# A transformer layer on one core: the last norm's scale and bias as matmuls, and expert 30's work in another order

## The chip, the cores and the metric

The kernel runs on one core of a Trainium2 chip. The metric is the device time of one execution in microseconds. Of the engines, PE is TensorE (matmuls and transposes; PEld is its weight load), DVE is VectorE, ACT is ScalarE, POOL is GpSimd, and SP is SyncE, which here does little but issue DMAs. All times below are in us from the start of the span of one profiled execution.

## The reference

One layer over 256 tokens of 1024 channels: `x = LayerNorm(a*x + HybridMixer(x))`, then `x = LayerNorm(a*x + MoE(x))`, in float32. Only the second half matters here:

```
logits = xf @ router_w + router_b            # 256 tokens, 32 experts
top_v, top_i = lax.top_k(logits, 4); gates = softmax(top_v)
# for every expert e, the tokens that chose it:
h = xblk @ w1[e] + b1[e]                     # 1024 -> 2048
gate, upv = split(h); gate = min(gate, 7); upv = clip(upv, -7, 7)
act = (upv + 1.0) * (gate * sigmoid(1.702 * gate))
y  += gates * (act @ w2[e] + b2[e])          # 1024 -> 1024
x = (x - mean) * rsqrt(var + eps) * ln2_g + ln2_b
```

Every expert's weights are read once: 8 MB of `w1` and 4 MB of `w2`, 32 times.

## The kernel before, in words

The first 260 us hold the mixer, the first norm and the router. Then the experts run in a Python loop that is unrolled, `e = 0..30`, with the last one, 31, written out behind it. An expert works on 64 slots. `gemm1` (L1090) multiplies the gathered tokens with `w1` into the PSUM banks `h0` and `h1`, 64 partitions for each half. `hs` is their copy in SBUF (ACT L1096, DVE L1097). `act_steps` (L1173) transposes `hs` on PE into a bank `u`, adds the bias on DVE (L1187), and forms the activation in four more steps on DVE and one on ACT (L1191 to L1196). `gemm2` (L1203) multiplies the result with `w2`; ACT copies it to `ys` (L1209). `scatter` (L1211) multiplies by the gates, transposed by `turn_slots` into `ext`, and adds into the four accumulator banks `acc[t][half]`, which hold the whole layer's output until the end.

Experts run one behind the other: the `gemm2` of expert e-1 and the `scatter` of e-2 stand between the steps of expert e. At `e == SUMS` (8), `residuals()` adds the scaled `x1` into `acc` and `gates_by_expert()` makes `GT`, the gates with the experts on the partitions. The term with `b2` is one product, `gated_biases`: `GT` times `b2r`, four matmuls into `acc`. Before the change it stands in expert 30, and `b2r` is loaded there (L1291).

The weights come through a ring of 23 buffers of 1 MB each. `new_w()` takes the next one; `load_w` (L75) issues one DMA from SP's queue. SP works in program order: a transfer waits until its buffer is free, and until the transfer eight before it has landed, since the queue's completions are counted on eight semaphores in rotation. Expert 31's transfers (class `Last`, L1157) are cut finer at the end: the last 2 MB of `w1` are four transfers of 512 KB, each with one half of the columns for k = 6 and 7, and the last 1 MB of `w2` is two.

PE and, where the code says `PE.`, `DVE.` or `ACT.`, the other engines keep program order (class `Pinned`, whose one call is L48: most rows of PE therefore carry that line, and the tile names tell them apart).

Behind expert 31, `add_sums` (L1386) takes the moments from `acc`, and `normed` (L1403) applies the norm: a mean and a standard deviation for each of two token blocks t, then four pieces (t, h) of 128 x 512. Three of them take two DVE instructions each. The fourth, (0, 1), takes one of ACT and two of POOL. Each piece is stored by one DMA of 256 KB (L1420).

`overflow` (L1227) then reads the largest count of tokens of any expert. Only if it is over 64 does a loop run that works on the crowded experts again and repeats the norm. Before the change this loop reads its weights in blocks into `rws`, one DMA for every matmul.

Of the kernel before, what the change touches and what calls it, by code (L numbers as in the profile page):

```python
# [9 lines left out]
F32 = mybir.dt.float32  # L10
# [5 lines left out]
OP = mybir.AluOpType  # L16
# [5 lines left out]
E = 32  # L22
# [29 lines left out]
def hybrid(ctx: ExitStack, tc: tile.TileContext, A, out, dbg=None):  # L52
# [884 lines left out]
    def u_tile():  # L937
        return ps.tile([128, 512], F32, name="u", bufs=2)
# [4 lines left out]
    def h_tile(c):  # L943
        return ps.tile([128, 512], F32, name=f"h{c}")
# [75 lines left out]

    hs = t1[:, :1024]
    hT = t1[:, 1024:].rearrange("p (j h s) -> p j h s", j=8, h=2)
    wblk = rws.rearrange("p v k e -> p (v k e)")
# [66 lines left out]
    def gemm1(xg, w1):  # L1090

        hp = [h_tile(c) for c in range(2)]
        for k, c, half in w1.order:
            PE.matmul(hp[c][half * 64:(half + 1) * 64], xg[:, k],
                             w1(k, half * 2 + c), start=(k == 0), stop=(k == 7), skip_group_check=True)
        nc.scalar.copy(hs[:, :512], hp[0])  # L1096
        nc.vector.tensor_copy(hs[:, 512:], hp[1])  # L1097

    class Weights:


        def __init__(self, e, one=False):
            self.e, self.one = e, one
            self.order = ([(k, c, half) for c in range(2) for half in range(2) for k in range(8)] if one else
                          [(k, c, half) for k in range(8) for c in range(2) for half in range(2)])

        def block(self, name, k, c):
            cs = slice(c * 512, (c + 1) * 512)
            if name == 'moe_w1':
                src = A[name][ds(self.e, 1), k * 128:(k + 1) * 128, cs]  # L1110
            else:
                src = w2v[ds(self.e, 1), :, k // 2, k % 2, cs]
            nc.sync.dma_start(wblk, src.rearrange("e p f -> p (e f)"))
            return wblk

    class First(Weights):
        def load(self):
            self.w = [load_w(w1v[self.e][:, k:k + 1, :], 1, 2048) for k in range(8)]
            return self

        def __call__(self, k, c):
            if self.one:
                return self.block('moe_w1', k, c)
            return self.w[k][:, 0, c * 512:(c + 1) * 512]

    class Second(Weights):
        def load(self):
            self.w = [load_w(w2v[self.e][:, q], 2, 1024) for q in range(4)]
            return self

        def __call__(self, k, c):
            if self.one:
                return self.block('moe_w2', k, c)
            return self.w[k // 2][:, k % 2, c * 512:(c + 1) * 512]

    class Last:
# [36 lines left out]
    def act_steps(bias, a, g=None, banks=None):  # L1173


        bv = bias.rearrange("p (h j) -> p j h", h=2)
        pieces = [slice(q * 4, (q + 1) * 4) for q in range(2)]
        js = slice(0, 8)
        if g is not None:
            js = slice(4 * g, 4 * g + 4)  # L1180
            pieces = [js]
        for i, piece in enumerate(pieces):
            n = piece.stop - piece.start
            p = (banks[i] if banks else u_tile())[:, :n * 128]
            for j in range(n):
                PE.transpose(p[:, j * 128:(j + 1) * 128], pair(hs, piece.start + j), ident)
            nc.vector.tensor_tensor(hT[:, piece], p.rearrange("p (j h s) -> p j h s", j=n, h=2),  # L1187
                                    bv[:, piece, :].unsqueeze(3).to_broadcast([128, n, 2, SLOTS]), op=OP.add)
        yield
        gate, up = hT[:, js, 0, :], hT[:, js, 1, :]  # L1190
        nc.vector.tensor_scalar(gate, gate, LIMIT, None, op0=OP.min)  # L1191
        sg = hs[:, js.start * 128:js.start * 128 + (js.stop - js.start) * 64].rearrange("p (j s) -> p j s", s=64)
        nc.scalar.activation(sg, gate, AF.Sigmoid, scale=1.702)
        nc.vector.tensor_scalar(up, up, LIMIT, -LIMIT, op0=OP.min, op1=OP.max)
        nc.vector.tensor_tensor(sg, sg, gate, op=OP.mult)
        nc.vector.scalar_tensor_tensor(a[:, js], up, 1.0, sg, op0=OP.add, op1=OP.mult)  # L1196

    def act(*args, **kw):
        for _ in act_steps(*args, **kw):
# [2 lines left out]

    def gemm2(a, w2):  # L1203
        yp = u_tile()
        for k, c, half in w2.order:
            if c == 0:
                PE.matmul(yp[half * 64:(half + 1) * 64, :], a[:, k], w2(k, half),
                                 start=(k == 0), stop=(k == 7), skip_group_check=True)
        nc.scalar.copy(ys, yp)  # L1209

    def scatter(gT, first=False):  # L1211
# [21 lines left out]
    def overflow(stores):  # L1233

        with ExitStack() as behind:
            for i in stores:
                behind.enter_context(tc.issue_after(i))
            most = nc.values_load(cnts[0:1, E:E + 1], min_val=0, max_val=T)
        with tc.If(most > SLOTS):
            with tc.For_i(0, E, 1) as ei:  # L1240
                ce = nc.values_load(cnts[0:1, ds(ei, 1)], min_val=0, max_val=T)
                with tc.If(ce > SLOTS):
                    be = lp.tile([128, 16], F32, name="be")
                    nc.vector.tensor_copy(be.unsqueeze(2), b1T[:, :, ds(ei, 1)])
# [37 lines left out]
    for e in range(E - 1):  # L1282
# [3 lines left out]
        w1 = First(e).load()  # L1286
        if 0 < e < E - 2:
            w2 = Second(e - 1).load()
        if e == E - 2:
            b2r = new_w()[:E, :D]  # L1290
            nc.sync.dma_start(b2r, A['moe_b2'])  # L1291
        if e:
# [17 lines left out]
        elif e < E - 2:  # L1310
# [17 lines left out]
            if e == SUMS:  # L1328
                scatter(*late)
                late = None  # L1330
                residuals()
                GT = gates_by_expert()
            if e == E - 3:

                scatter(*late)
                gemm2(a, Second(e).load())
        else:
            gT = turn_slots(buf, u_tile())
            scatter(prev[1])
            steps = act_steps(b1T[:, :, e], a_main)  # L1340
            next(steps)
            gTn = turn_slots(1 - buf, h_tile(0), S)

            gated_biases(GT, b2r)
            for _ in steps:
                pass
            a = a_main
            w2 = Second(e).load()
            last = Last().load()
            gemm2(a, w2)  # L1350
# [47 lines left out]
                          start=False, stop=True, skip_group_check=True)  # L1398
        add_sums(st, c)
    ov = out[0].rearrange("(t p) d -> p t d", p=128)  # L1400
    y = new_w().rearrange("p (t d) -> p t d", t=2)

    def normed(st):  # L1403
        stats = [statistics(st[t]) for t in range(2)]
        nm = lp.tile([128, 1], F32, name="nm")

        def norm2(t, h, tail=None):
            (mu, rs), c = stats[t], slice(h * 512, (h + 1) * 512)
            d = y[:, t, c]
            out_q = nc.sync  # L1410
            if tail is None:
                out_q = nc.scalar
# [3 lines left out]
            else:  # L1416
# [3 lines left out]
            return out_q.dma_start(ov[:, t, c], d).ins  # L1420

        def scales():
            for _, rs in stats:
                DVE.reciprocal(rs, rs)
            DVE.scalar_tensor_tensor(nm, stats[0][0], -1.0, stats[0][1], op0=OP.mult, op1=OP.mult)

        return [norm2(0, 0, scales), norm2(0, 1)] + [norm2(1, h, lambda: None) for h in range(2)]

    overflow(normed(st))

# [22 lines left out]
```

## Time and profile before

| | us |
|---|---|
| median of 3 runs | 1203.75 |
| the runs | 2316.03, 1203.75, 1200.88 |
| the profiled execution's own time | 1199.88 |
| its span (first to last instruction) | 1198.0 |
| busy: PE, DVE, ACT, POOL | 1134.0, 347.0, 208.2, 64.4 |
| DMA | 449.37 MB, mean 375 GB/s |

Busy times are sums over the whole span, which has stages with different limits, so the table says little by itself. The chain of waits, followed back from the last instruction, names DMA for 51% and PE for 45% of the span. Matmul ends are modelled, so a PE that reads as busy all the time may hold short waits.

### The profile page before, as it was taken

Reading aid. Unit: us, or ns where it says so; the run is one execution under the profiler, and the core shown is the slowest. Engines: PE = TensorE matmul, PEld = TensorE weight load, DVE = VectorE, ACT = ScalarE, POOL = GpSimd, SP = SyncE. Lnnn points to the kernel's source line nnn. Section 1 sums busy time; section 2 is a strip of 40 time slices with the busy share of each in tenths; the row PEclk is TensorE's granted clock in tenths of the full one; section 3 lists DMA queues with packets and bytes.
Section 4 is the critical chain, followed back from the end, with each engine's and each line's share of the span. In section 5 each row is a group of like instructions: output and inputs, shape, how many; then the busy total and the mean of one; then the engine's idle time right before and its main releaser. Section 6 shows DMA issues by size and latency. Waiting matters only on the chain.

```text
span 1198.0 us, 15607 instructions
## 1 busy us (share of the span) xinstructions
PE 1134.0 (95%) x6464; PEld 584.8 (49%) x6465; DVE 347.0 (29%) x700; ACT 208.2 (17%) x491; POOL 64.4 (5%) x106
## 2 busy tenths in 40 slices
PE   8999999999999999999999898989898989899994
PEld 7998889984434334343433333333333333334332
DVE  6679777472112111111121111111111111111014
ACT  5115554532101011010101000101010101011001
POOL 1010001311000000000000000000000000000000
PEclk9999999999999999999999999999999999999998
DMA  9994466869999999999999999999999999999993
GB/s 247 327 321 142 129 205 250 306 231 419 424 424 424 424 425 423 425 423 425 423 425 422 426 423 425 423 424 423 426 423 425 424 424 425 425 424 425 419 406 153
DMA packets 100358, 449.37 MB, mean 375 GB/s; under 512 B 11108, under 2 KB 44826, under 8 KB 51514
## 3 DMA queue, kind: packets, MB, share of 16 engines
q1 hardware_dynamic: 99774, 447.51, 92.6%
q8 instruction: 52, 0.85, 0.3%
q10 hardware_dynamic: 508, 0.81, 0.2%
q14 instruction: 24, 0.20, 0.1%
HBM read 447.25 MB, written 1.05 MB: 374 GB/s over the span
## 4 chain that ended last, share of the span: by engine, by line
DMA 51%; PE 45%; DVE 2%; SPq 1%; ACT 1%; issue 0%; ACTq 0%; DVEq 0%
DMA w<-in_moe_w_dram 50%; PE h L48 16%; PE u L48 8%; PE mm L87 4%; PE mm L88 4%; PE mm L89 4%; PE acc L48 3%; DMA w<-in_w_in_dram 1%; PE sc L641 1%; PE yps L686 1%; PE ptp L677 1%; PE sc L48 1%; PE mm L48 1%; DVE w L48 0%; DMA x<-in_x_dram 0%
## 5 line engine op out<-in xcount | busy, mean ns | idle before, releaser
L48 PE MATMUL h<-w,t 128*64 128x512 f32 (+1 forms) x1472 | 328.0, 588 | 31.2 <-DMA w<-in_moe_w_dram 30.4
L48 PEld LDWEIGHTS h<-w,t 128*64 128x64 f32 x1472 | 99.4, 136 | 249.0 <-issue 161.4
L48 PE MATMUL u<-w,t 128*64 128x512 f32 x960 | 212.9, 595 | 0.0
L1097 DVE COPY t<-h 128x512 f32<-128x512 f32 x31 | 21.4, 691 | 512.8 <-PE h L48 512.8
L48 PE MATMUL h<-w,rws 128*64 128x512 f32 x640 | 146.2, 603 | 11.2 <-DMA w<-in_moe_w_dram 11.0
L48 PEld LDWEIGHTS u<-w,t 128*64 128x64 f32 x960 | 66.2, 137 | 124.4 <-issue 118.3
L48 PEld LDWEIGHTS h<-w,rws 128*64 128x64 f32 x640 | 43.8, 138 | 108.7 <-issue 76.1
L87 PE MATMUL mm<-xh,ws 128*128 128x256 f32 x336 | 96.8, 288 | 0.0
L1096 ACT COPY t<-h 128x512 f32<-128x512 f32 x31 | 18.1, 585 | 447.5 <-PE h L48 447.5
L88 PE MATMUL mm<-xl,ws 128*128 128x256 f32 x336 | 95.0, 283 | 0.0
L89 PE MATMUL mm<-xh,ws 128*128 128x256 f32 x336 | 94.9, 283 | 0.0
L82 DVE TENSOR_TENSOR ws<-w,ws 128x1024 fp32r<-128x1024 f32 (+1 forms) x64 | 73.2, 1148 | 11.8 <-ACT ws L81 11.0
L1074 POOL TENSOR_TENSOR ext<-ext,G 128x128 f32<-128x128 f32 x62 | 27.1, 456 | 815.8 <-PE h L48 797.2
L48 PE MATMUL acc<-t,ext 64*128 64x512 f32 (+1 forms) x264 | 63.9, 602 | 1.6 <-ACT t L1393 0.9
L87 PEld LDWEIGHTS mm<-xh,ws 128*128 128x128 f32 x336 | 64.3, 191 | 1.0 <-issue 0.8
L88 PEld LDWEIGHTS mm<-xl,ws 128*128 128x128 f32 x336 | 64.4, 192 | 0.0
L89 PEld LDWEIGHTS mm<-xh,ws 128*128 128x128 f32 x336 | 64.3, 191 | 0.0
L1196 DVE SCALAR_TENSOR_TENSOR t<-t 128x512 f32<-128x512 f32 (+1 forms) x32 | 21.6, 675 | 144.0 <-PE u L48 143.8
L1209 ACT COPY t<-u 128x512 f32<-128x512 f32 x31 | 18.2, 586 | 175.3 <-PE u L48 175.3
L1187 DVE TENSOR_TENSOR t<-u,b1T 128x512 f32<-128x512 f32 x35 | 24.0, 690 | 78.3 <-PE u L48 78.3
L48 PEld LDWEIGHTS acc<-t,ext 64*128 64x128 f32 x264 | 22.7, 186 | 41.1 <-issue 27.8
L81 DVE CAST ws<-w 128x1024 fp32r<-128x1024 f32 (+1 forms) x47 | 29.7, 642 | 23.0 <-PE mm L89 15.6
(338 smaller groups left out, 1085.6 us busy)
## 6 DMA issues: line engine op xcount, KB each, us to landing
w<-in_moe_w_dram SPq DMA_DIRECT2D x381, 1024.0 KB
w<-in_w_in_dram SPq DMA_DIRECT2D x22, 1024.0 KB
w<-in_w_up_dram SPq DMA_DIRECT2D x6, 1024.0 KB
w<-in_cmp_w_dram SPq DMA_DIRECT2D x4, 1024.0 KB
w<-in_w_o_dram SPq DMA_DIRECT2D x4, 1024.0 KB
w<-in_w_in_dram SPq DMA_DIRECT2D x6, 512.0 KB
w<-in_moe_w_dram SPq DMA_DIRECT2D x6, 512.0 KB
out_dram<-w SPq DMA_DIRECT2D x3, 256.0 KB
```

The costliest lines, as they stand in the source:

```text
L48: return lambda *a, **k: self.tc.keep_in_program_order(f(*a, **k))
L81: copy(hi, src)
L82: return sub.tensor_tensor(lo, src, hi.bitcast(F32), op=OP.subtract).ins
L87: pe.matmul(p, ah, bh, start=first, stop=False, **kw)
L88: pe.matmul(p, ah, bl, start=False, stop=False, **kw)
L89: pe.matmul(p, al, bh, start=False, stop=last, **kw)
L1074: nc.gpsimd.tensor_tensor(SG[:, t], S[:, t, x:x + 1].to_broadcast([128, 2, SLOTS]), gsrc[:, t].unsqueeze(2).to_broadcast([128, 2, SLOTS]), ...
L1096: nc.scalar.copy(hs[:, :512], hp[0])
L1097: nc.vector.tensor_copy(hs[:, 512:], hp[1])
L1187: nc.vector.tensor_tensor(hT[:, piece], p.rearrange("p (j h s) -> p j h s", j=n, h=2), bv[:, piece, :].unsqueeze(3).to_broadcast([128, n, ...
L1196: nc.vector.scalar_tensor_tensor(a[:, js], up, 1.0, sg, op0=OP.add, op1=OP.mult)
L1209: nc.scalar.copy(ys, yp)
```

## The change

It has four parts.

1. The closing norm. Each bank that holds a piece of the result is first filled with the bias row by a matmul of the identity with `b2`; DVE forms `(acc - mean) * g2` for each piece; a matmul with a diagonal matrix of the inverse deviations scales it and adds it to the bank; ACT (and DVE for a quarter) copies the bank to SBUF. `y` lies in `t1` and no longer in a ring buffer. The last piece is copied and stored in two halves, so there are five stores, all from SP's queue, and none from ACT's. POOL has no work in it any more.
2. Expert 30. The transposes of `act_steps` stand ahead of the scatter of expert 29; the activation is made in two halves; the `gated_biases` are no longer here.
3. Expert 8. `b2r` is loaded here, and `gated_biases` stands here, behind `residuals()`.
4. The crowded experts load their weights through the ring, with the same `load()` as the others.

```diff
-        for k, c, half in w1.order:
-            PE.matmul(hp[c][half * 64:(half + 1) * 64], xg[:, k],
-                             w1(k, half * 2 + c), start=(k == 0), stop=(k == 7), skip_group_check=True)
+        for k in range(8):
+            for c in range(2):
+                for half in range(2):
+                    PE.matmul(hp[c][half * 64:(half + 1) * 64], xg[:, k],
+                              w1(k, half * 2 + c), start=(k == 0), stop=(k == 7), skip_group_check=True)
...
-                        gemm1(xg[0], First(ei, True))
+                        gemm1(xg[0], First(ei).load())
                         a = act(be, xg[0])
-                        gemm2(a, Second(ei, True))
+                        gemm2(a, Second(ei).load())
...
-        if e == E - 2:
+        if e == SUMS:
             b2r = new_w()[:E, :D]
             nc.sync.dma_start(b2r, A['moe_b2'])
...
-                GT = gates_by_expert()
+                gated_biases(gates_by_expert(), b2r)
...
             gT = turn_slots(buf, u_tile())
+            a = a_main
+            steps = [act_steps(b1T[:, :, e], a, c, DVE) for c in range(2)]
+            for c in range(2):
+                next(steps[c])
             scatter(prev[1])
-            steps = act_steps(b1T[:, :, e], a_main)
-            next(steps)
             gTn = turn_slots(1 - buf, h_tile(0), S)
-
-            gated_biases(GT, b2r)
-            for _ in steps:
-                pass
-            a = a_main
+            for c in range(2):
+                for _ in steps[c]:
+                    pass
...
-    y = new_w().rearrange("p (t d) -> p t d", t=2)
+    y = t1.rearrange("p (t d) -> p t d", t=2)
 
     def normed(st):
+
+        banks = [[u_tile(), u_tile()], [h_tile(0), h_tile(1)]]
+        for t in range(2):
+            for h in range(2):
+                PE.matmul(banks[t][h], ident, b2[:, h * 512:(h + 1) * 512], start=True, stop=False,
+                          skip_group_check=True)
         stats = [statistics(st[t]) for t in range(2)]
...
-                ACT.activation(d, acc[t][h], AF.Identity, bias=nm, scale=rs)
-                nc.gpsimd.tensor_tensor(d, d, g2[:, c], op=OP.mult)
-                nc.gpsimd.tensor_tensor(d, d, b2[:, c], op=OP.add)
...
-                DVE.scalar_tensor_tensor(d, acc[t][h], mu, g2[:, c], op0=OP.subtract, op1=OP.mult)
-                tail()
-                DVE.scalar_tensor_tensor(d, d, rs, b2[:, c], op0=OP.mult, op1=OP.add)
...
+        def centered(t, h):
+            c = slice(h * 512, (h + 1) * 512)
+            DVE.scalar_tensor_tensor(y[:, t, c], acc[t][h], stats[t][0], g2[:, c], op0=OP.subtract, op1=OP.mult)
+
+        def scaled(t, h, n, copies):
+            for i, copy in enumerate(copies):
+                c = slice(h * 512 + i * n, h * 512 + (i + 1) * n)
+                p = banks[t][h][:, i * n:(i + 1) * n]
+                PE.matmul(p, diag[t], y[:, t, c], start=False, stop=True, skip_group_check=True)
+                copy(y[:, t, c], p)
+                stores.append(nc.sync.dma_start(ov[:, t, c], y[:, t, c]).ins)
+
+        centered(0, 0)
+        for t in range(2):
+            rs = stats[t][1]
+            DVE.reciprocal(rs, rs)
+            DVE.tensor_scalar(diag[t], ident, rs, None, op0=OP.mult)
+        for t, h in ((0, 1), (1, 0), (1, 1)):
+            centered(t, h)
+        for t, h in ((0, 0), (0, 1), (1, 0)):
+            scaled(t, h, 512, [ACT.copy])
+        scaled(1, 1, 256, [DVE.tensor_copy, ACT.copy])
+        return stores
```

PE's order in expert 30, from the gates' transposes behind `gemm1` to `gemm2`. `t_3267` holds `ys` and the activation, `t_3268` holds `hs`, `ext` the gates, `acc_*` are the four accumulators. Before:

```order
L48 MATMUL u<-ident,ext 128x128 x2
L48 MATMUL acc_3275<-t_3267,ext 128x512
L48 MATMUL acc_3276<-t_3267,ext 128x512
L48 MATMUL acc_3466<-t_3267,ext 128x512
L48 MATMUL acc_3467<-t_3267,ext 128x512
L48 MATMUL u<-ident,t_3268 128x128 x8
L48 MATMUL h_7042<-ident,ext 128x128 x2
L48 MATMUL acc_3275<-w,GT 128x512
L48 MATMUL acc_3276<-w,GT 128x512
L48 MATMUL acc_3466<-w,GT 128x512
L48 MATMUL acc_3467<-w,GT 128x512
L48 MATMUL u<-w,t_3267 64x512 x16
```

The same place now, in the changed kernel, on PE:

```order
L48 MATMUL u<-ident,ext 128x128 x2
L48 MATMUL u<-ident,t_3268 128x128 x8
L48 MATMUL acc_3275<-t_3267,ext 128x512
L48 MATMUL acc_3276<-t_3267,ext 128x512
L48 MATMUL acc_3466<-t_3267,ext 128x512
L48 MATMUL acc_3467<-t_3267,ext 128x512
L48 MATMUL h_7046<-ident,ext 128x128 x2
L48 MATMUL u<-w,t_3267 64x512 x16
```

The eight transposes of `hs` moved ahead of the four scatter matmuls, and the four matmuls with `GT` are gone from here. They stand in expert 8 now, where PE's order reads (`x_76` with `ident_a` are the residuals, `G` the gates):

```order
L48 MATMUL acc_3275<-x_76,ident_a 128x512
L48 MATMUL acc_3276<-x_76,ident_a 128x512
L48 MATMUL acc_3466<-x_76,ident_a 128x512
L48 MATMUL acc_3467<-x_76,ident_a 128x512
L48 MATMUL u<-ident,G 32x128 x2
L48 MATMUL acc_3275<-w,GT 128x512
L48 MATMUL acc_3276<-w,GT 128x512
L48 MATMUL acc_3466<-w,GT 128x512
L48 MATMUL acc_3467<-w,GT 128x512
```

PE runs these four right behind the transposes of `G`, and expert 9's `gemm1` follows them. At the end of the program PE's order is now this, where before the four scatter matmuls of 256 columns were its last work:

```order
L48 MATMUL acc_3275<-t_3267,ext 128x256
L48 MATMUL acc_3276<-t_3267,ext 128x256
L48 MATMUL acc_3466<-t_3267,ext 128x256
L48 MATMUL acc_3467<-t_3267,ext 128x256
L48 MATMUL u<-w,ident 128x512 x2
L48 MATMUL h_7231<-w,ident 128x512
L48 MATMUL h_7232<-w,ident 128x512
L48 MATMUL u<-t_3268,ext 128x512 x2
L48 MATMUL h_7231<-t_3268,ext 128x512
L48 MATMUL h_7232<-t_3268,ext 128x256 x2
```

Behind the last scatter stand four matmuls that put the bias in, and then the scaling ones: three of 512 columns and two of 256.

## Rows read from the trace of the kernel before

**Rows 1.** The page's second part: the span in 40 equal slices of 30 us. DMA is the mean busy share of the 16 DMA engines in tenths (9 is 90% or more), GB/s what they moved.

```profile
DMA  9994466869999999999999999999999999999993
GB/s 247 327 321 142 129 205 250 306 231 419 424 424 424 424 425 423 425 423 425 423 425 422 426 423 425 423 424 423 426 423 425 424 424 425 425 424 425 419 406 153
```

**Rows 2.** The chain that ended last, in order of time: start, length, what.

```profile
499.44 5.62 PE acc L48 x16
...
533.23 19.71 DMA w<-in_moe_w_dram
...
1119.05 20.30 DMA w<-in_moe_w_dram
...
1145.00 3.62 PE acc L48 x8
...
1160.99 8.86 PE h L48 x40
...
1191.11 0.98 DVE w L48
```

**Rows 3.** Waits from 533 to 1139 us, of SP's queue and of PE: who waited, for whom, us in total, times, longest.

```profile
SPq L75 <- DMA w<-in_moe_w_dram: 507.3, 243, 2.9
SPq L75 <- PE h L48: 3.5, 12, 0.4
...
PE h L48 <- DMA w<-in_moe_w_dram: 40.4, 80, 0.7
```

**Rows 4.** SP's queue near the end: start and length of three issues by the timeline, and the semaphore waits of the stores' line, which begin at 1167.9.

```profile
1155.41 1.45 SPq L1157 DMA_DIRECT2D w<-in_moe_w_dram  x1
...
1165.30 0.66 SPq L1157 DMA_DIRECT2D w<-in_moe_w_dram  x1
1166.58 0.55 SPq L1157 DMA_DIRECT2D w<-in_moe_w_dram  x1
...
L1420 SPq EVENT_SEMAPHORE  x3: 17/17/17, 1167.9 to 1190.8; - x3
```

**Rows 5.** PE's timeline in expert 31's `gemm1`: k = 0 and 1 (16 records), the scatter of expert 30 (8), then k = 2 to 5 with both column halves and k = 6, 7 with the first (40 records). A float32 matmul leaves two records.

```profile
1155.47 3.60 PE L48 MATMUL h<-w,t 128*64 128x512 f32 x16
1159.01 1.99 PE L48 MATMUL acc<-t,ext 64*128 64x512 f32 x8
1160.92 8.91 PE L48 MATMUL h<-w,t 128*64 128x512 f32 x40
```

**Rows 6.** Two stretches near the end: length, then for PE, PEld, DVE, ACT and POOL the busy time and the count, then the granted clock, the DMA share and GB/s.

```profile
1166.00:1170.00 4.00, 3.84 (x18) 1.32 (x14) 0.00 (x0) 0.13 (x1) 0.00 (x0) 1.00 1.03 411
...
1178.00:1180.00 2.00, 2.00 (x22) 1.24 (x20) 0.13 (x1) 0.00 (x0) 0.00 (x0) 1.00 0.36 126
```

**Rows 7.** The timeline in expert 8 (the residuals, the copy of `GT`) and the starts of two `gemm1` that lie two experts apart.

```profile
501.36 3.70 PE L48 MATMUL acc<-x,ident_a 128*128 128x512 f32 x8
505.32 0.41 DVE L1224 COPY GT<-u 32x256 f32<-32x256 f32 x1 [5.82 <-PE u L48]
...
531.60 13.96 PE L48 MATMUL h<-w,t 128*64 128x512 f32 x64
...
583.55 13.95 PE L48 MATMUL h<-w,t 128*64 128x512 f32 x64
```

**Rows 8.** The timeline of the activation: the transposes of expert 30, and, of expert 31, which is done in halves before too, the bias, the sigmoid and the last step of one half.

```profile
1143.56 1.23 PE L48 MATMUL u<-ident,t 128*128 128x128 f32 x8
...
1171.29 0.69 DVE L1187 TENSOR_TENSOR t<-u,b1T 128x512 f32<-128x512 f32 x1 [23.03 <-PE u L48]
...
1172.43 0.42 ACT L1193 ACTIVATE t<-t 128x256 f32<-128x256 f32 x1 [1.97 <-DVE t L1191]
...
1173.34 0.43 DVE L1196 SCALAR_TENSOR_TENSOR t<-t 128x256 f32<-128x256 f32 x1
```

**Rows 9.** The timeline of the end: an ACT copy of 512 columns and one of 256 from PSUM, the last scatter, the end of the moments, the first piece's subtraction, the last store.

```profile
1169.87 0.58 ACT L1366 COPY t<-h 128x512 f32<-128x512 f32 x1 [13.60 <-PE h L48]
...
1183.66 0.37 ACT L1393 COPY t<-h 128x256 f32<-128x256 f32 x1 [2.25 <-PE h L48]
...
1184.09 1.14 PE L48 MATMUL acc<-t,ext 64*128 64x256 f32 x8 [0.47 <-ACT t L1393]
...
1186.16 0.38 DVE L48 BATCH_NORM_AGGREGATE bn_mv<-st 128x2 f32<-128x24 f32 x2
...
1186.69 0.75 DVE L48 SCALAR_TENSOR_TENSOR w<-acc,bn_mv,w 128x512 f32<-128x512 f32 x1
...
1192.11 0.33 SPq L1420 DMA_DIRECT2D out_dram<-w  x1
```

**Rows 10.** SP behind the last store: its wait at the branch, and the nine semaphores that it goes through after it (shortest/median/longest ns, first and last start).

```profile
SPq L1239 <- SPq L1239: 2.5, 1, 2.5
...
L1239 SPq EVENT_SEMAPHORE  x9: 17/17/17, 1196.1 to 1196.7; - x9
```

**Rows 11.** Three stretches in the columns of Rows 6; the granted clock is the third number from the right.

```profile
1082.00:1086.00 4.00, 4.00 (x30) 2.93 (x26) 0.69 (x1) 1.76 (x3) 0.00 (x0) 1.00 1.01 426
1086.00:1090.00 4.00, 4.00 (x13) 1.27 (x14) 0.00 (x0) 0.58 (x1) 0.00 (x0) 0.57 1.02 424
...
1188.00:1190.00 2.00, 0.00 (x0) 0.00 (x0) 1.97 (x3) 0.52 (x1) 1.32 (x2) 0.62 0.34 131
```

**Rows 12.** The page's sixth part, the stores that SP issued in the whole execution.

```profile
out_dram<-w SPq DMA_DIRECT2D x3, 256.0 KB
```

More of the change, by code (lines that the diff above doesn't have):

```diff
@@ L1022, in hybrid @@
     hT = t1[:, 1024:].rearrange("p (j h s) -> p j h s", j=8, h=2)
-    wblk = rws.rearrange("p v k e -> p (v k e)")
     a_main = t2[:, 1024:1536].rearrange("p (j s) -> p j s", j=8)
@@ L1096, in gemm1 @@
         nc.scalar.copy(hs[:, :512], hp[0])
         nc.vector.tensor_copy(hs[:, 512:], hp[1])
[L1099 to L1114, printed above, removed]
@@ L1116, in hybrid, with of_expert, __init__ @@
-    class First(Weights):
+    def of_expert(v, e):
+        return v[e] if isinstance(e, int) else v[ds(e, 1)].rearrange("e p r f -> (e p) r f")
+    class First:
+        def __init__(self, e):
+            self.src = of_expert(w1v, e)
         def load(self):
-            self.w = [load_w(w1v[self.e][:, k:k + 1, :], 1, 2048) for k in range(8)]
+            self.w = [load_w(self.src[:, k:k + 1, :], 1, 2048) for k in range(8)]
             return self
         def __call__(self, k, c):
-            if self.one:
-                return self.block('moe_w1', k, c)
@@ L1124, in __call__, with __init__ @@
             return self.w[k][:, 0, c * 512:(c + 1) * 512]
-    class Second(Weights):
+    class Second:
+        def __init__(self, e):
+            self.src = A['moe_w2'][e] if isinstance(e, int) else A['moe_w2'][ds(e, 1)].rearrange("e f d -> (e f) d")
+            self.src = self.src.rearrange("(q p r) d -> q p r d", p=128, r=2)
         def load(self):
-            self.w = [load_w(w2v[self.e][:, q], 2, 1024) for q in range(4)]
+            self.w = [load_w(self.src[q], 2, 1024) for q in range(4)]
@@ L1129, in load @@
             return self
         def __call__(self, k, c):
-            if self.one:
-                return self.block('moe_w2', k, c)
             return self.w[k // 2][:, k % 2, c * 512:(c + 1) * 512]
@@ L1171, in second, with act_steps @@
                           start=(j == 0), stop=(j == 7), skip_group_check=True)
-    def act_steps(bias, a, g=None, banks=None):
+    def act_steps(bias, a, g=None, vec=nc.vector, banks=None):
         bv = bias.rearrange("p (h j) -> p j h", h=2)
@@ L1186, in act_steps @@
                 PE.transpose(p[:, j * 128:(j + 1) * 128], pair(hs, piece.start + j), ident)
-            nc.vector.tensor_tensor(hT[:, piece], p.rearrange("p (j h s) -> p j h s", j=n, h=2),
+            vec.tensor_tensor(hT[:, piece], p.rearrange("p (j h s) -> p j h s", j=n, h=2),
                                     bv[:, piece, :].unsqueeze(3).to_broadcast([128, n, 2, SLOTS]), op=OP.add)
@@ L1190, in act_steps @@
         gate, up = hT[:, js, 0, :], hT[:, js, 1, :]
-        nc.vector.tensor_scalar(gate, gate, LIMIT, None, op0=OP.min)
+        vec.tensor_scalar(gate, gate, LIMIT, None, op0=OP.min)
         sg = hs[:, js.start * 128:js.start * 128 + (js.stop - js.start) * 64].rearrange("p (j s) -> p j s", s=64)
         nc.scalar.activation(sg, gate, AF.Sigmoid, scale=1.702)
-        nc.vector.tensor_scalar(up, up, LIMIT, -LIMIT, op0=OP.min, op1=OP.max)
-        nc.vector.tensor_tensor(sg, sg, gate, op=OP.mult)
-        nc.vector.scalar_tensor_tensor(a[:, js], up, 1.0, sg, op0=OP.add, op1=OP.mult)
+        vec.tensor_scalar(up, up, LIMIT, -LIMIT, op0=OP.min, op1=OP.max)
+        vec.tensor_tensor(sg, sg, gate, op=OP.mult)
+        vec.scalar_tensor_tensor(a[:, js], up, 1.0, sg, op0=OP.add, op1=OP.mult)
     def act(*args, **kw):
@@ L1204, in gemm2 @@
         yp = u_tile()
-        for k, c, half in w2.order:
-            if c == 0:
+        for k in range(8):
+            for half in range(2):
                 PE.matmul(yp[half * 64:(half + 1) * 64, :], a[:, k], w2(k, half),
-                                 start=(k == 0), stop=(k == 7), skip_group_check=True)
+                          start=(k == 0), stop=(k == 7), skip_group_check=True)
         nc.scalar.copy(ys, yp)
@@ L1400, in hybrid @@
     ov = out[0].rearrange("(t p) d -> p t d", p=128)
-    y = new_w().rearrange("p (t d) -> p t d", t=2)
+    y = t1.rearrange("p (t d) -> p t d", t=2)
     def normed(st):
-        stats = [statistics(st[t]) for t in range(2)]
[L1405 to L1412, printed above, removed]
-                ACT.activation(d, acc[t][h], AF.Identity, bias=nm, scale=rs)
-                nc.gpsimd.tensor_tensor(d, d, g2[:, c], op=OP.mult)
-                nc.gpsimd.tensor_tensor(d, d, b2[:, c], op=OP.add)
-            else:
-                DVE.scalar_tensor_tensor(d, acc[t][h], mu, g2[:, c], op0=OP.subtract, op1=OP.mult)
-                tail()
-                DVE.scalar_tensor_tensor(d, d, rs, b2[:, c], op0=OP.mult, op1=OP.add)
[L1420 to L1427, printed above, removed]
@@ new lines, in normed @@
+        banks = [[u_tile(), u_tile()], [h_tile(0), h_tile(1)]]
[3 more added lines that the diff above has]
+                          skip_group_check=True)
+        stats = [statistics(st[t]) for t in range(2)]
+        diag = [ext[:, 512 + t * 128:640 + t * 128] for t in range(2)]
+        stores = []
+        def centered(t, h):
+            c = slice(h * 512, (h + 1) * 512)
+            DVE.scalar_tensor_tensor(y[:, t, c], acc[t][h], stats[t][0], g2[:, c], op0=OP.subtract, op1=OP.mult)
```

## The prediction

> **What bounds the kernel now.** I began with the page's slices. From about 290 us on, the DMA engines are busy in every slice at 420 to 425 GB/s, and only the last slice falls off [rows 1]. The expert stage is thus fed by a stream of weights that is never idle. The chain of waits then says who ends it [rows 2]. Up to 533 PE is on the chain, in expert 8 too (499.44). From 533.23 the chain runs on landings of weights, one after the other, until 1139.35 (1119.05 + 20.30). Behind that it is PE without a break, then DVE at the very end. So by the chain the last 52 us belong to PE, and work taken from PE there should shorten the kernel.
>
> I do not trust that reading, because a chain shows one path and hides a second one that is as long. So I looked at when the weights of expert 31 land. SP may not issue a transfer before the one eight places earlier has landed, so its issue times are landing times. The two last issues, at 1165.30 and 1166.58, mark the landing of w1 for k = 5 and of the first piece of k = 6, 7; the first store's semaphore wait at 1167.9 marks the second piece [rows 4]. PE reaches that second piece in its block that starts at 1160.92: 40 records in 20 pairs; the 0.59 us of one record's own length off the 8.91, over 19 steps, is 0.44 a pair, and the 17th pair starts at 1160.92 + 16 x 0.44 = 1167.9 [rows 5]. **PE and the stream arrive at the same moment.** The stream itself is full there, with a share of 1.03 at 1166 to 1170, and still moves weights at 1178 to 1180 [rows 6]. The kernel has two bounds in its last 52 us, level with each other, and the change shortens one of them.
>
> **The change, part by part.** *Expert 30.* The four `GT` matmuls go: 3.62 us of PE's chain [rows 2]. The transposes come before the scatter, so the activation runs beside it. PE then has: transposes 1.23 from about 1141.7 [rows 8], a scatter of 1.9 (1159.01 to 1160.92, [rows 5]), 0.3 of gate transposes, free at about 1145.1. The first half of the activation starts as its four transposes end, at about 1142.4. DVE adds both biases (2 x 0.69), and from there to the half's last step it is about 1.7 us, as in expert 31: bias done at 1172.0, last step over at 1173.34 + 0.43 [rows 8]. So it is ready at about 1145.5 and `gemm2` starts there, instead of 1145.00 + 3.62 = 1148.6. PE gains 3.1 us. That is the whole gain on offer, and it lasts until PE meets the stream. w1 for k = 1 landed at 1155.41 [rows 4]; PE, 3.1 us early, would want it at 1154.1 (half of the 3.60-us block behind 1155.47 - 3.1, [rows 5]) and loses 1.3 us to it. Pieces k = 2 to 5 take the next part, and k = 6 is the end: with or without the gain PE starts it at 1167.9. I take **0.0 us** (bounds: 3.1 less if PE's side were the only one; nothing more).
>
> *Expert 8.* PE gets the same four matmuls, which by the residuals, of the same size, are 3.70 less an overlap, say 3.5 [rows 7], and waits for the copy of `GT`, 0.41 [rows 7], with two handovers: about 4.2 in all. This is while PE is on the chain. But two `gemm1` two experts apart start 52.0 us apart [rows 7], 26.0 each, while an expert's 12 MB take 12 x 1.0486 MB / 424 GB/s = 29.7. PE gains 3.7 us an expert on the stream, so it is back at the stream's heels little more than one expert later, and then waits for it 40.4 us in all up to 1139 [rows 3]. That is the cover: 0. If it were gone, 4.2. The ring is no obstacle either: between 533 and 1139 SP waited 507.3 us on landings and 3.5 on PE [rows 3], so buffers come free in time. `b2r` is 0.13 MB; it leaves the stream at expert 30 and joins it at expert 8, where it is as full [rows 1]: 0, at best 0.3 (0.13 MB / 424 GB/s) if it falls into a gap.
>
> *The closing norm.* Before: moments end at about 1186.5, the last store is issued at 1192.11 [rows 9]. Now PE carries four bias matmuls behind the last scatter, and the scaling of 4 x 512 columns behind them. The nearest row is the residuals, 128 x 128 on 512 columns in float32, four in 3.70 with the drain and about 3.5 without [rows 7]. The scatter ends at 1184.09 + 1.14 = 1185.2 [rows 9]; 3.5 + 3.7 make 1192.4. DVE is not late: from 1186.6 four subtractions at 0.75 and some small steps end near 1190.2, and the diagonal is there before the bias is in. Behind the last quarter stands an ACT copy of 256 columns at 0.37 and two handovers [rows 9]: the last store goes out at 1192.8, **0.7 us later**. ACT's copies of 512 columns at 0.58 keep pace with PE's 0.9. The waits for ring semaphores ahead of DVE's first subtraction go with `y`, which frees DVE and not PE. Bounds: PE's bias matmuls wholly hidden, about -2.8; PE at half its clock, +7.2 (a rival below).
>
> *After the last store* SP reads the count and branches; it stands 2.5 us at the branch and leaves it at 1196.1 [rows 10], 4.0 after its issue. I move this with the issue. [...]
>
> *The crowded experts.* SP issued three stores in the whole execution [rows 12]; the loop would have issued more. It doesn't run, before or after: 0.
>
> **Sum:** 1199.9 + 0.0 + 0.0 + 0.7 = 1200.6 against the profiled execution. The two runs near it that had no profile, 1200.88 and 1203.75, lie 1.0 and 3.9 above; I add 1.0 and forecast **1201.5 us**, against a median before of 1203.75 which is the higher of them. About 2% (24 us) is what a measurement of this kernel can tell from no change; no part here comes near it.
>
> **The rivals.** *A, PE's side alone sets the end.* Then the 3.1 us go through: 1201.5 - 3.1 = 1198.4. For it speaks the chain, on PE from 1139.35 on [rows 2]; against it the semaphore at 1167.9 [rows 4]. It would decide if in other executions the weights of k = 6 landed 3 us sooner. 0.14.
>
> [...] From 1086 to 1090 the granted clock was 0.57, most of it at the lower level, behind a stretch of narrow matmuls [rows 11] that by the records had PE busy all the time. The tail before the norm has narrow matmuls and short waits too. If the clock falls as the bias matmuls begin, 7.2 us of them become 14.4: 1208.7. It decides if the clock falls before 1192; until now it fell at 1188 to 1190, with PE idle since 1185.2 [rows 9, 11], which the new work prevents. 0.06. [...]
>
> *C, slower: the 4.2 us at expert 8 stay.* PE is on the chain there, and if the ring were short the stream would stop for it: 1205.7. Against it SP's 3.5 us [rows 3]. 0.05.
>
> The forecast's own case gets 0.72; 0.03 is left for things of which no row speaks.
>
> **Range and chances.** The forecast with the scatter of the runs (1200 to 1204.5) and A reach from 1197.5; C reaches to 1205.5. B is left out. All named cases lie within 2%: same 0.95, faster 0.02, slower 0.03.
>
> **What would show it.** Expert 30: transposes ahead of the scatter, `gemm2` about 3 us earlier against the last landing of expert 30's w1. Then PE waits for weights in expert 31, before k = 1 and before k = 6, about 3 us in sum, and the chain of waits goes on DMA up to about 1168. The norm: PE on the chain for 7 us behind the last scatter, at a clock of 1.00, POOL with nothing. Expert 8: a landing on the chain one or two experts later than 533. I am wrong if PE shows no such waits and the span is near 1195, if the clock falls in the norm, or if the last store goes out earlier against the last scatter than before.

## The result and the profile after

| | before | after |
|---|---|---|
| median of 6 runs each, us | 1200.90 | 1208.46 |
| ratio, 95% interval | | 1.0061 [1.0048, 1.0074] |
| profiled execution: its own time, its span, us | 1199.88, 1198.0 | 1208.99, 1207.2 |
| share of the chain: PE, DMA | 45%, 51% | 53%, 44% |

(The ratio leaves out one run of before, of 2316 us, which the median of six still counts.) The change is called "same" at 2%, but it is 7.6 us slower, more than twice what its interval is wide. 1201.5 was forecast, with a range up to 1205.5. The page's slices of the changed kernel already show where the time went:

```profile
DMA  8994466769999999999999999999999999999993
GB/s 243 319 324 141 126 203 251 304 235 420 420 422 420 421 420 421 408 420 420 422 420 421 421 422 420 421 420 421 421 420 421 421 420 420 421 421 421 421 413 142
```

The stream of weights is as unbroken as in [rows 1], but between its ends it moves 420 to 422 GB/s, in one slice 408, where it moved 422 to 426. A table of two stretches says it with more weight (length, then busy time and count of PE, PEld, DVE, ACT and POOL, then granted clock, DMA share, GB/s). After:

```profile
300.00:450.00 150.00, 149.89 (x754) 60.87 (x752) 25.85 (x45) 16.28 (x36) 5.31 (x12) 1.00 1.01 421
...
500.00:1100.00 600.00, 558.82 (x2680) 212.51 (x2678) 87.11 (x152) 57.21 (x125) 17.69 (x40) 0.99 1.01 421
```

and the same stretches of the kernel before:

```profile
300.00:450.00 150.00, 149.88 (x754) 60.84 (x752) 25.82 (x45) 16.29 (x36) 5.31 (x12) 1.00 1.01 424
...
500.00:1100.00 600.00, 560.41 (x2700) 212.24 (x2698) 86.35 (x151) 56.64 (x124) 17.71 (x40) 1.00 1.01 424
```

From 300 to 450 us both kernels execute the same instructions: what the change moves begins behind that. The engines' busy times and counts agree, the DMA share is 1.01 in both, and yet the stream is slower by 3 GB/s. So no instruction that the change adds, drops or moves is the cause.

What it is worth is read from SP's queue (start, length, line, count). In the changed kernel the first weights of the experts and the last two transfers of expert 31's `w2` are issued here (the first of these two waits for the landing of `w1` for k = 5, eight places earlier):

```profile
195.61 1.31 SPq L75 DMA_DIRECT2D w<-in_moe_w_dram  x3
```

```profile
1173.69 1.85 SPq L1147 DMA_DIRECT2D w<-in_moe_w_dram  x2
```

Before, the second place is at 1165.30 [rows 4], and the first here:

```profile
194.04 1.30 SPq L75 DMA_DIRECT2D w<-in_moe_w_dram  x3
```

The stream begins 1.6 us later and ends 8.4 us later, so from the first place to the second it takes 978.1 us instead of 971.3, 6.8 more. From about 290 to 1165 us, 3 of 424 GB/s are 875 x 3 / 424 = 6.2 us, and the view rounds these rates to 1 GB/s. The load of `b2r` in expert 8, which makes one slice 408, has no part in it: after_pad below loads `b2r` there too, and its stream takes 971.3 us. The 1.6 lies in the mixer, where the kernels below scatter: they have that first issue anywhere from 193.3 to 196.8, and the latest is one with a fast stream (after_bd256).

Behind the stream the chain of waits is the one that the prediction described (start, length, what):

```profile
1132.82 19.90 DMA w<-in_moe_w_dram
1152.78 20.89 DMA w<-in_moe_w_dram
1173.72 4.61 PE h L48 x16
...
1192.56 1.13 PE acc L48 x8
1193.70 1.91 PE u L48 x4
1195.61 1.72 PE h L48 x4
1197.33 1.72 PE u L48 x4
1199.04 1.30 PE h L48 x4
1200.85 0.71 PE h L48 x2
```

Before, the last landing on it ended at 1139.35 and PE had the rest [rows 2]. Now landings hold it until 1173.67 (in after_pad below until 1165.65), and PE starts k = 5 of expert 31 the moment they end, with k = 6 and 7 behind it. The whole delay of the stream thus reaches the end.

### The profile page after: what moved, and what is told of

Read it like the earlier page. It is cut to its first block, busy times and chain, and to the rows that moved or that the text cites. A ratio compares the mean times of both kernels' runs of the same rounds, so it can differ in the third digit from the quotient of the medians.

```text
span 1207.2 us, 15641 instructions
## 1 busy us (share of the span) xinstructions
PE 1146.2 (95%) x6482; PEld 590.2 (49%) x6483; DVE 345.8 (29%) x704; ACT 209.6 (17%) x495; POOL 61.0 (5%) x104
## 4 chain that ended last, share of the span: by engine, by line
PE 53%; DMA 44%; DVE 1%; ACT 0%; issue 0%; SPq 0%; ACTq 0%; DVEq 0%
DMA w<-in_moe_w_dram 43%; PE h L48 20%; PE u L48 10%; PE mm L87 4%; PE mm L88 4%; PE mm L89 4%; PE acc L48 3%; DMA w<-in_w_in_dram 1%; PE sc L641 1%; PE yps L686 1%; PE mm L48 1%; PE ptp L677 1%; PE sc L48 1%; PE ptp L48 0%; DMA x<-in_x_dram 0%; PE ptp L87 0%
```

## The experiments

**Where the 3 GB/s went.** The norm no longer makes one small tile, and that is the only thing I found that the change alters for the work before 450 us:

```diff
-        nm = lp.tile([128, 1], F32, name="nm")
```

The tile has 4 bytes a partition and takes 32. Its pool, `late`, lies at the right end of SBUF and is filled from there, so everything to the left of it moves up by 32 bytes: the buffers of `ring_x` (203520 to 203552, bytes from a partition's start), `t2` and `t1`, and those of `ring_c` (146176 to 146208). All of them began at multiples of 256 bytes. Of the 23 buffers of the ring, 5 are `ring_c`, 2 `ring_x`, 8 `ring_a` (start 128 behind a multiple of 256 in both kernels), and 4 each `ring_b` and `ring_d` (64 behind in both). My theory was that these starts set the speed of the stream; the rival, that some part of the new order does. Two kernels put the question both ways: the changed kernel with an unused tile in the old one's place, and the kernel before with one tile more.

```diff
     lp = ctx.enter_context(tc.tile_pool(name="late", bufs=1, side="right"))
+    lp.tile([128, 1], F32, name="pad")
```

On the change (after_pad):

> The changed kernel with one unused tile of 4 bytes a partition (32 with its padding) in the pool at the right end of the SBUF. It puts the seven ring buffers of the pools ring_c and ring_x, and t1 and t2, back to the addresses of the kernel before (multiples of 256 bytes instead of 32 bytes behind one); nothing else differs from the change. Theory (addresses): the stream of weights goes back from 421 to 424 GB/s between 500 and 1100 us, its last landing comes some 8 us sooner, and the time is 1200 to 1201.5 us, ratio to before 0.999 to 1.001, with the closing norm's 0.7 us the only thing left. Rival (the work itself: b2r and the four matmuls in expert 8, or the norm, slow the stream): it stays at 1208, ratio 1.006, and 421 GB/s.

On the kernel before (before_off32):

> The kernel before with one more unused tile of 32 bytes a partition in the same pool, so that ring_c, ring_x, t1 and t2 lie 32 bytes below a multiple of 64, with none of the change's work. Theory (addresses): 1207 to 1209 us, ratio 1.006, at 421 GB/s between 500 and 1100 us. Rival (the work itself): 1200.9 us, ratio 1.000, at 424 GB/s.

Then the same place moved by 64 bytes (`lp.tile([128, 56], F32, name="pad")` in the changed kernel, after_off64), and all 23 buffers put at multiples of 256 (after_all256: after_pad with a tile of 128 bytes ahead of `ring_a` and one of 64 in the constants):

```diff
+    front = ctx.enter_context(tc.tile_pool(name="front", bufs=1, side="left"))
+    front.tile([128, 32], F32, name="pad_a")
     ring_a = ctx.enter_context(tc.tile_pool(name="ring_a", bufs=NA, side="left"))
...
+    consts.tile([128, 16], F32, name="pad_b")
```

> The changed kernel with 224 bytes a partition of unused tile in the same pool: ring_c and ring_x then begin 64 bytes behind a multiple of 256, as ring_b and ring_d do in every kernel so far. If 64 bytes are what counts: as with the 32-byte tile, 1200 to 1201.5 us, 424 GB/s. If 256 bytes count, 1206 to 1209 us, about 421 GB/s. Rival (the work itself): 1208.

> The changed kernel with the 32-byte tile and two more unused tiles (128 bytes ahead of ring_a, 64 bytes in the constants), so that all 23 ring buffers begin at multiples of 256 bytes; in the kernel before ring_a begins at 128 and ring_b and ring_d at 64 behind one. If 64 bytes are what counts: as with the 32-byte tile alone, 1200 to 1201.5 us. If 256 bytes count: the stream gets faster than before, 426 to 428 GB/s, and the time is 1192 to 1198 us, ratio 0.993 to 0.998.

All eleven kernels, with the starts of the buffers in bytes behind a multiple of 256, the GB/s from 500 to 1100 us, and the ratio to the kernel before on the same chip. They were timed on three chips, so kernels are compared by their ratios; the medians of two chips are not on one scale.

| kernel | a | b, d | c | x | GB/s | median us (runs) | ratio [95%] |
|---|---|---|---|---|---|---|---|
| (before) | 128 | 64 | 0 | 0 | 424 | 1200.90 (6) | 1 |
| (after) | 128 | 64 | 32 | 32 | 421 | 1208.46 (6) | 1.0061 [1.0048, 1.0074] |
| after_pad | 128 | 64 | 0 | 0 | 424 | 1200.77 (11) | 0.9994 [0.9985, 1.0003] |
| before_off32 | 128 | 64 | 224 | 224 | 421 | 1207.39 (4) | 1.0047 [1.0032, 1.0063] |
| after_off64 | 128 | 64 | 64 | 64 | 421 | 1207.10 (4) | 1.0049 [1.0033, 1.0064] |
| after_all256 | 0 | 0 | 0 | 0 | 427 | 1192.98 (4) | 0.9927 [0.9912, 0.9942] |
| norm_alone | 128 | 64 | 0 | 0 | 424 | 1202.76 (11) | 1.0009 [0.9999, 1.0019] |
| expert30_alone | 128 | 64 | 0 | 0 | 424 | 1200.26 (11) | 0.9992 [0.9983, 1.0001] |
| after_bd256 | 128 | 0 | 0 | 0 | 427 | 1195.11 (4) | 0.9947 [0.9932, 0.9962] |
| expert30_all256 | 0 | 0 | 0 | 0 | 427 | 1193.05 (5) | 0.9932 [0.9919, 0.9946] |
| before_all256 | 0 | 0 | 0 | 0 | 427 | 1195.13 (5) | 0.9940 [0.9926, 0.9953] |
| all32 | 32 | 224 | 32 | 32 | 420 | 1209.97 (4) | 1.0065 [1.0050, 1.0080] |
| c32_alone | 128 | 64 | 224 | 0 | 422 | 1205.47 (10) | 1.0028 [1.0017, 1.0038] |

The rows of the stretch behind that column, in the columns used above; before_off32, after_pad and after_all256:

```profile
500.00:1100.00 600.00, 554.86 (x2668) 209.74 (x2666) 87.05 (x152) 57.27 (x125) 17.75 (x40) 1.00 1.01 421
```

```profile
500.00:1100.00 600.00, 562.29 (x2700) 213.77 (x2702) 86.37 (x151) 56.70 (x124) 17.73 (x40) 1.00 1.01 424
```

```profile
500.00:1100.00 600.00, 567.96 (x2731) 217.34 (x2728) 87.61 (x153) 57.23 (x125) 17.69 (x40) 0.99 1.01 427
```

One unused tile takes the slowdown from the changed kernel, the same tile brings it to the kernel before, and the DMA share is 1.01 in all three: it does not tell a slow stream from a fast one. The counts of PE (2668, 2700, 2731 records in the same 600 us) follow the stream, though only roughly over all the kernels. That the 32 bytes by which `ring_c`, `ring_x`, `t1` and `t2` moved cost the 7.6 us is shown; which of them do it is the next question.

**How much of it, and where.** Three more kernels move other rings, or one ring alone. after_bd256 is after_pad with an unused tile of 192 bytes in the constants (`consts.tile([128, 48], F32, name="pad_b")`), which brings `ring_b` and `ring_d` to multiples of 256 and leaves the others where they are. In all32 every buffer is off (`front.tile([128, 40], F32, name="pad_a")` in the changed kernel). In c32_alone, made from after_pad, a pool of its own shifts `ring_c` alone:

```diff
     t2, t1 = [late2.tile([128, 2048], F32, name=v) for v in ("t2", "t1")]
+    gap = ctx.enter_context(tc.tile_pool(name="gap", bufs=1, side="right"))
+    gap.tile([128, 1], F32, name="pad_c")
```

> The changed kernel with the 32-byte tile, and ring_b and ring_d moved from 64 to 0 bytes behind a multiple of 256; ring_a stays at 128. If every buffer off 256 costs alike (16 buffers made 7.8 us), half of it comes: 1196 to 1198 us. If a start at 128 costs as little as one at 0, nearly all of it comes: 1193 to 1194.5 us.

> The changed kernel as it is (ring_c and ring_x at 32 bytes behind a multiple of 256) with 160 bytes of unused tile ahead of ring_a: ring_a then begins at 32, ring_b and ring_d at 224 behind one. If the cost goes by buffer and start, from the runs so far 1.1 us for a buffer at 32, 0.9 at 224: 1193 + 15 x 1.1 + 8 x 0.9 = 1216.7 us, that is 1213 to 1220, some 417 GB/s. If only a mixture of starts in the ring costs, and not the starts themselves: 1208 or less.

> The changed kernel with the 32-byte tile and one more of 32 bytes between t1, t2 and ring_c: of all the tiles, the five buffers of ring_c alone begin 32 bytes below a multiple of 64 (224 behind one of 256); ring_x, t1 and t2 lie where they lay before. If it is the buffers that the stream writes: 5 x 0.9 = 4.5 us over the 1200.8 of the kernel with one tile, 1204.5 to 1206. If it is where t1 and t2 lie, which the engines work on: 1200.8.

c32_alone came out as the theory of the buffers has it, at 1205.5. after_bd256, at 1195.1, fell between its two ranges. all32 missed: I had the cost grow with every buffer that is off, and it does not; it is not at the rival's 1208 either. Rows of c32_alone and all32:

```profile
500.00:1100.00 600.00, 558.97 (x2684) 212.39 (x2686) 86.38 (x151) 56.64 (x124) 17.68 (x40) 1.00 1.01 422
```

```profile
500.00:1100.00 600.00, 556.99 (x2676) 211.28 (x2674) 86.39 (x151) 56.69 (x124) 17.74 (x40) 1.00 1.01 420
```

By the ratios, against after_pad's 0.9994: `ring_c` alone, five buffers, costs 0.34% (4.1 us); with `ring_x`, `t1` and `t2` it is 0.55% (after_off64) and 0.67% (after), or 0.47% in the kernel before, against its own 1 (before_off32); with everything off 0.71% (8.5 us). From the other end, eight buffers from 64 to 0 gain 0.47% (5.6 us), and eight more from 128 to 0 gain 0.20% (2.4 us). The intervals are some 0.15% to either side, so by the times 32, 64 and 224 behind can't be told apart.

The length of the stream, between the two places named above, tells more. In the kernel before and the three others that leave the ring where it was it takes 971.3 to 971.5 us. With seven buffers moved it takes 978.1 (after), 978.0 (before_off32) or 977.1 (after_off64), with `ring_c` alone 975.8, with everything off 980.3. In after_bd256 the two places are

```profile
196.83 6.91 SPq L75 DMA_DIRECT2D w<-in_moe_w_dram  x5
...
1162.66 1.84 SPq L1149 DMA_DIRECT2D w<-in_moe_w_dram  x2
```

and in after_all256

```profile
193.38 6.92 SPq L77 DMA_DIRECT2D w<-in_moe_w_dram  x5
...
1158.71 1.78 SPq L1151 DMA_DIRECT2D w<-in_moe_w_dram  x2
```

which makes 965.8 and 965.3 us, one execution each. Eight buffers moved from 64 to 0 are worth 5.5 us of stream, and eight from 128 to 0 only 0.5: 128 behind costs next to nothing here, and the rest of the 2.4 us is not in the stream. That 64 behind is slow says that a multiple of 64 is not enough.

The runs show that the start matters, here on the side that is written: with `ring_c` and `ring_x` at 0 the stretch from 500 to 1100 us moves 424 GB/s (after_pad), with both at 64 behind 421 (after_off64). Whether a multiple of 128 would do they do not settle, though 0.5 us of stream for eight buffers speaks for it. Why the start matters stays open.

**The parts by themselves.** With the buffers in their old places, norm_alone is after_pad with experts 8 and 30 as they were, and expert30_alone is the kernel before with the new order of expert 30 and `gated_biases` in expert 8:

```diff
-        if e == E - 2:
+        if e == SUMS:
...
-                GT = gates_by_expert()
+                gated_biases(gates_by_expert(), b2r)
```

> The new closing norm alone: expert 30 and expert 8 as before, and the 32-byte tile, so that all ring buffers lie where they lie in the kernel before. Theory of the prediction: the last scatter comes when it came, the last store 0.7 to 1.5 us later against it, of which the end behind the store may give 0.7 back; 1200.9 to 1202.5 us, ratio 1.000 to 1.0015. Rival (PE's and DVE's parts overlap better than I reckoned): ratio 0.997 to 0.999, some 2 us less.

> The reordered expert 30 and the moved biases alone, with the old norm and all ring buffers where they lie before. Theory of the prediction (the stream is level with PE): the second matmul of expert 30 comes 3.1 us earlier, PE then waits some 3 us for weights in expert 31, and the time is that of before, ratio 0.999 to 1.0005. Rival (PE's side alone sets the end): ratio 0.9975, 3 us less.

The norm costs 1.1 us by its ratio, though its interval just takes in none (the median, 1202.76, lies just above the range, the ratio within it); the rest is nothing either way. Last, the kernel before and expert30_alone with all buffers at multiples of 256:

> The kernel before, none of the change's work, with two unused tiles (128 bytes ahead of ring_a, 64 bytes in the constants) that put all 23 ring buffers at multiples of 256 bytes. Addresses theory: the same 7 to 8 us less that the changed kernel gained so, 1192.5 to 1194 us, ratio 0.993, 427 GB/s; the change is then worth nothing beside it (1193.0 with the change, 1193.1 with expert 30's part alone). Rival (the changed work is what lets the aligned buffers pay): 1196 or more.

> The reordered expert 30 and the moved biases with the old norm, and all 23 ring buffers at multiples of 256 bytes. By the addresses theory this is the changed kernel with aligned buffers less what the new norm costs: 1191.5 to 1193.5 us, ratio 0.992 to 0.994, at 427 GB/s. Rival (the new norm is worth something once the stream is faster): 1194 or more.

before_all256 came out a little above what I expected, at 1193.7 to 1197.2, while expert30_all256 lies within 1193.0 to 1193.2. The chain of before_all256's profile tells why:

```profile
1113.14 20.32 DMA w<-in_moe_w_dram
...
1139.09 4.42 PE acc L48 x8
1143.51 9.57 PE u L48 x32
```

and the stretch around them:

```profile
1141.00:1149.00 8.00, 8.00 (x19) 2.08 (x19) 1.32 (x2) 0.00 (x0) 0.00 (x0) 0.57 1.02 428
```

The clock falls while the four `GT` matmuls run. They take 4.42 us on the chain, where it was 3.62 before [rows 2]; the granted clock from 1141 to 1149 is 0.57; and `gemm2` takes 9.57 us, where the same matmuls took 7.02 in the kernel before (at 1148.62 on its chain). norm_alone's profile shows the same (9.76), so part of its 1.1 us may be this and not the norm. By its chain PE's side sets the end of before_all256 from 1133.46 on, so there it counts. In expert30_all256 these matmuls are gone from the tail and landings are on the chain until 1158.56. By the ratios its order gains 0.08%, 1.0 us (the medians, of two chips, differ by 2.1), and the two intervals overlap; I call that likely, not shown. Both kernels with the new expert 30 and all buffers at multiples of 256, at 1193, are faster than before and after; between the old and the new norm no difference is to be seen there (ratios 0.9932 and 0.9927).

## Why the prediction was wrong

**The step that failed** is in the part on what bounds the kernel, carried into the sum: "The expert stage is thus fed by a stream of weights that is never idle", and then "an expert's 12 MB take 12 x 1.0486 MB / 424 GB/s = 29.7". I read 424 GB/s as full because the share was 1.0, and took it over into the changed kernel. It is the speed of one layout. In the changed kernel it is 421, in another 427, at the same share. The sum has no term for it: I costed the instructions of the norm, and did not ask what its small tile `nm` held in place. The moved buffers were worth 5.6 us by the ratio of before_off32, 8.0 by those of after and after_pad, and 6.7 by the length of the stream in either pair. Because I had rightly found that the stream sets the end, I could have said that any change of its speed goes through undiminished: 0.7% of 875 us.

**Expert 30: right.** The timeline of the changed kernel (start, length, tile, count, wait before it):

```profile
1147.79 1.94 PE L48 MATMUL h<-w,t 128*64 128x512 f32 x8 [0.55 <-DMA w<-in_moe_w_dram]
...
1149.93 1.40 PE L48 MATMUL u<-ident,t 128*128 128x128 f32 x8
...
1151.27 1.99 PE L48 MATMUL acc<-t,ext 64*128 64x512 f32 x8
...
1153.81 6.66 PE L48 MATMUL u<-w,t 128*64 128x512 f32 x30 [0.19 <-PE h L48]
```

`gemm2` starts 6.0 us behind the last block of `gemm1`; before it was 1148.62 - 1139.40 = 9.2. The gain of 3.1 to 3.2 us is as worked out, and so is its end: PE waits for the stream again. In expert 31 it does so before k = 0, k = 1 and k = 5:

```profile
1161.31 1.94 PE L48 MATMUL h<-w,t 128*64 128x512 f32 x8 [0.41 <-DMA w<-in_moe_w_dram]
1163.72 1.94 PE L48 MATMUL h<-w,t 128*64 128x512 f32 x8 [0.47 <-DMA w<-in_moe_w_dram]
...
1173.72 4.59 PE L48 MATMUL h<-w,t 128*64 128x512 f32 x16 [0.57 <-DMA w<-in_moe_w_dram]
```

That is 1.4 us, and within the last block PE's weight loads wait another 1.0, in two waits, for the pieces of k = 6 and 7 (its 16 records take 4.59 us, where 16 took 3.60 without a wait [rows 5]): 2.4 us in sum (2.1 in after_pad), where about 3 was foretold, "before k = 1 and before k = 6". The term 0.0 holds: expert30_alone is at 0.9992. **Rival A**, PE's side alone, did not come in: expert30_alone, which has this gain and not the new norm, would have had to be 3.1 us faster than before, and its interval ends at 0.9983 (2.0 us).

**Expert 8: the cover right, the price too low.** The timeline and the stretch behind it:

```profile
507.08 0.41 DVE L1214 COPY GT<-u 32x256 f32<-32x256 f32 x1 [5.82 <-PE u L48]
...
507.54 4.93 PE L48 MATMUL acc<-w,GT 32*128 32x512 f32 x8 [0.50 <-DVE GT L1214]
```

```profile
510.00:517.00 7.00, 7.00 (x15) 1.76 (x16) 0.00 (x0) 0.00 (x0) 0.00 (x0) 0.52 1.01 419
```

In this execution the clock fell while these matmuls ran and was granted at 0.52 from 510 to 517, so the four matmuls took 4.93 us and expert 9's `gemm1` 16.02 by the chain, where 13.96 is usual [rows 7]. With the copy that is 0.5 + 4.9 + 2.1 = 7.5 us, not 4.2. In after_pad the matmuls took 3.69. It is absorbed in both. The first long run of landings on the chain begins at 627.46 (604.45 in after_pad, 533.23 before), so with 26 us of PE an expert it took some three to four experts more, and not "little more than one"; the times show nothing of it. **Rival C** is out.

**The norm: the size right, by two errors.** The end of the changed kernel, where the last scatter starts, and the last two pieces:

```profile
1192.56 1.13 PE L48 MATMUL acc<-t,ext 64*128 64x256 f32 x8 [0.47 <-ACT t L1383]
...
1193.63 1.98 PE L48 MATMUL u<-w,ident 128*128 128x512 f32 x4
...
1195.45 1.88 PE L48 MATMUL h<-w,ident 128*128 128x512 f32 x4
...
1198.88 1.45 PE L48 MATMUL h<-t,ext 128*128 128x512 f32 x4
...
1200.37 0.42 DVE L48 COPY t<-h 128x256 f32<-128x256 f32 x1 [1.79 <-PE h L48]
...
1200.85 0.70 PE L48 MATMUL h<-t,ext 128*128 128x256 f32 x2 [0.52 <-DVE t L48]
1201.64 0.37 ACT L48 COPY t<-h 128x256 f32<-128x256 f32 x1 [1.12 <-PE h L48]
```

The stores' issues (shortest/median/longest ns, first and last start):

```profile
L1414 SPq DMA_DIRECT2D out_dram<-t x5: 332/344/409, 1198.8 to 1202.0; - x5
```

The last store is issued at 1202.0, 9.5 us behind the start of the last scatter; before it was 1192.11 - 1184.09 = 8.0 [rows 9]. So this part is +1.5 and not +0.7. Most of the difference is a wait of 0.52 us that I left out: both halves of the last piece lie in one PSUM bank, and in the row at 1200.85 PE waits for DVE's copy of the first before it writes the second. **Rival B**, the closing matmuls at half the clock (from 1086.5 to 1089.5 it read 0.50 in the kernel before), did not happen: the granted clock from 1193 to 1201 is 1.00.

Behind the last store I moved the old 5.9 us (1198.0 - 1192.11) along unchanged. It became 1207.2 - 1202.0 = 5.2. SP's own wait at its branch, 2.5 us before [rows 10], is at most 1.0 now; the last branch to end is PE's, at 1205.4 (in the same columns):

```profile
L1229 SPq EVENT_SEMAPHORE  x9: 17/17/17, 1203.8 to 1205.3; - x9
...
L1229 PEldq COMPARE_BRANCH  x1: 3978/3978/3978, 1201.4 to 1201.4; - x1
```

Before, PE's was short:

```profile
L1239 PEldq COMPARE_BRANCH  x1: 352/352/352, 1184.7 to 1184.7; - x1
```

There PE was done 6 us earlier than the others. Together +1.5 - 0.7 = +0.8 for a term of 0.7: the size came out right by luck, since what I left out at either end nearly cancels. norm_alone's +1.1 us agrees, as far as its interval goes.

The chances put 0.95 on a change within 2%, and it is within 2%. But the range had no case for a stream whose speed changes, and that is the case that came. Two slips in its sums change nothing: 1200.6 and 1.0 make 1201.6, and rival C's 1205.7 lies outside the range that C is said to reach to.

## What to carry to other kernels

Where a stream of transfers sets the end, look at where its buffers start in memory, before and after a change: a tile that appears or disappears in a pool shifts what lies beyond it, and a DMA share of 1.0 does not say that the stream is as fast as it can be (here it read 1.01 at 420, at 424 and at 427 GB/s). Align the buffers of such a stream on purpose (here to 256 bytes, by two or three unused tiles, which gained 0.6 to 0.7% over the kernel before), and put an unused tile in the place of a removed one before crediting or blaming anything else. A stretch in which two kernels execute the same instructions, compared by GB/s, shows this at once, and the time between two issues of SP that bound the stream measures it more finely than the runs' times do.

## What the runs showed of the hardware

- Loads of 1 MB into 128 partitions ran at 427 GB/s with all 23 buffers at multiples of 256 bytes, at 427 too with eight of them 128 behind (0.5 us more over the whole stream), at 424 with eight 128 and eight 64 behind, at 421 with the other seven off too, at 420 with all 32 or 224 behind; the share of the DMA engines reads 1.01 each time. Why the loss does not add up buffer by buffer stays open, and so does what `ring_x` and what `t1` and `t2` cost by themselves: that was not tried.
- The granted clock fell to 0.52 and 0.57 while the four `GT` matmuls ran, in expert 8 (510 to 517) or in expert 30 (1141 to 1149 in before_all256), and not in every profile: in after_pad they took 3.69 us in expert 8, in the kernel before 3.69 us in expert 30, there at a granted clock of 1.00 (1144.9 to 1148.6). PE read as busy through each of these stretches; in expert 8 it had waited 0.50 us before the first of these matmuls. It read as busy at 1086 too, where the clock was 0.57 [rows 11]. What brings the clock down was not tried.
- A branch on PE took 3.98 us behind the norm's matmuls in the changed kernel, and 0.35 us in the kernel before, which does not have these; one execution each. Why was not tried.
